# One gate product in plain fp32, and mixed rows made at another time, in the projections of an RWKV-7 layer

## The chip, the cores and the metric

The kernel runs on 1 core of one Trainium2 chip. The time is device microseconds of one execution; the median of the runs counts.

## The reference

A two-layer encoder trunk, 512 tokens by 1024 channels, in fp32: each layer is a feed-forward block, a token mixer (attention in layer 0, RWKV-7 in layer 1) and another feed-forward block. The change lies in the projections ahead of RWKV-7's scan. What they compute, cut:

```python
xx = 0.5 * (x_prev + x_next) - x
xr, xw, xk, xv, xa, xg = (x + xx * mix[i] for i in range(6))
r = xr @ w_rkv[0]; k = xk @ w_rkv[1]; v = xv @ w_rkv[2]
wl = w0 + einsum(tanh(einsum(xw, w1)), w2)          # decay, two directions
a  = sigmoid(a0 + einsum(einsum(xa, a1), a2))       # learning rate, two directions
g  = sigmoid(xg @ g1) @ g2                          # gate; g1 is 1024 x 160
kk = k * k_k / norm over each head of (k * k_k)
```

## The kernel before, in words

Everything is channel-major: 1024 channels are 8 chunks of 128 partitions, 512 tokens lie along the free axis. Large products are done as three: a matrix is split into a high half (`fp32r`, ScalarE's copy) and a low half (raw minus high, on VectorE for activations, mostly on GpSimd for weights), and `mm3` (L225 to L227) adds high x high, high x low, low x high. A few small products are plain fp32 matmuls.

`rwkv_project` works in this order, on one instruction queue per engine:

- `first` (L622 to L632), hand-ordered on ScalarE and VectorE: for each chunk VectorE adds the neighbours (`add`, L622), subtracts x (L626: `xx`) and mixes the keys' rows (L615, `mix`); ScalarE copies the high half into `xT` (L629), VectorE makes the low half (L632).
- keys: for each of 8 chunks a weight row block is loaded and split (`load_rows`, L189, L220, L221 on GpSimd) and multiplied into 8 PSUM banks, 24 products a chunk (lines L225 to L227, out `bank`, in `xT` and `ring` or `w`). TensorE's order is that of the code.
- `low_rank(0, w1, 1)` mixes the decay's rows ("w rows", L615 into `ring`), `low_rank(1, a1, 4)` the learning rate's ("a rows"); `rank(n)` (L610) multiplies each by its 1024 x 128 matrix in plain fp32.
- ScalarE evacuates each key bank (`store`, L639, into a rotation of 4 and later 8 buffers, stored to DRAM as `d_k`) and squares it (L670); L684 sums the squares by head in plain fp32 (16 columns), VectorE takes the reciprocal (L688).
- `raws(0)` mixes r's rows into the 4 `tmp` buffers (L646), stores them (`d_xr`, L647) and multiplies the first 128 columns of r (L692, plain fp32). `raws(3)` mixes v's rows and stores them (`d_xv`).
- `decays(z)` (w2, 24 products each; ScalarE L709, VectorE L710, stored as `d_lw`), between the two the gate's first product: `mixed(5)` mixes and splits the gate's rows into `xT` (L615, L220, L221), 24 `mm3` products with g1's first 128 columns and 24 with its last 32 (`g1b`).
- the gate's second product (48 products) and its stores `d_g`; then the scan begins: loads of `tri`, `k`, `iv`, `r`, `lw`, `e` (the rate's rank product from `d_ah`), with `lw` needed by the scan's first product (L1228) and `e` by its second (`ah`, L225).

Outside the hand-ordered pieces, a scheduler with its own time model orders VectorE, ScalarE, GpSimd and the DMA queue of SP; `behind(ins)` says that what is emitted in it is issued after `ins`. VectorE and SP are strict queues in the order shown below.

Of the kernel before, what the change touches and what calls it, by code (L numbers as in the profile page):

```python
# [10 lines left out]
F32 = mybir.dt.float32  # L11
BF16 = mybir.dt.bfloat16
F32R = mybir.dt.float32r
I32 = mybir.dt.int32
AF = mybir.ActivationFunctionType
ALU = mybir.AluOpType
AX = mybir.AxisListType

P = 128
# [4 lines left out]
ND = D // P  # L24
# [62 lines left out]
def halves_of(ap):  # L87
    return ap.rearrange("p (h t) -> p h t", h=2)
# [10 lines left out]
class Trunk:  # L99
# [473 lines left out]
    def rwkv_project(self, dram, xraw, w_rkv, w1, w2, a1, g1, g2, heads):  # L573

        nc = self.nc
        with self.pool("rwa") as pool:
# [9 lines left out]
            mixes = [self.new_xT()]  # L586
            rows = [[q[:, c, :] for q in (quarters(), quarters()) for c in range(4)] for _ in range(2)]
# [4 lines left out]
                ev[0] = (ev[0] + 1) % (4 * len(evs))  # L592
                return evs[ev[0] // 4][:, ev[0] % 4, :]

            def mixed(i):
                m = mixes[0]
                for c in range(ND):
                    raw = mix(i, c)
                    self.split(*m.get(c), halves_of(raw))
                return m  # L600

            def low_rank(n, w, i):
                nc.sync.dma_start(ranks[:, n], w.rearrange("(c p) f -> p c f", p=P))
                for c in range(ND):
                    mix(i, c, rows[n][c])

            def rank(n):
                pp = self.bank()
                for c in range(ND):
                    nc.tensor.matmul(pp, ranks[:, n, c, :], rows[n][c], start=c == 0, stop=c == ND - 1)  # L610
                return pp

            def mix(i, c, raw=None):
                raw = self.tmp() if raw is None else raw
                nc.vector.scalar_tensor_tensor(raw, xx[c], self.col(C_MIX + i, c),  # L615
                                               xraw[:, c, 1 : S + 1], ALU.mult, ALU.add)
                return raw

            def first(i):

                m = mixes[0]
                add = lambda c: nc.vector.tensor_tensor(xx[c], xraw[:, c, 0:S], xraw[:, c, 2 : S + 2], ALU.add)  # L622
                with self.tc.manual_schedule(engines=MANUAL_NORM):
                    add(0)
                    for c in range(ND):
                        nc.vector.scalar_tensor_tensor(xx[c], xx[c], 0.5, xraw[:, c, 1 : S + 1], ALU.mult, ALU.subtract)  # L626
                        raw = mix(i, c)
                        h, l = m.get(c)
                        hi = nc.scalar.activation(h, halves_of(raw), AF.Copy).ins  # L629
                        if c < ND - 1:  # L630
                            add(c + 1)
                        nc.vector.tensor_tensor(l, halves_of(raw), h.bitcast(F32), ALU.subtract)  # L632
                        if c == 0:
                            marks = hi, self.mark(l.bitcast(F32)[:, 0, 0:1])
                return m, marks

            def store(dst, src):
                t = evac()
# [3 lines left out]
            def raws(i, dst):  # L642

                for c in range(ND):
                    t = self.tmp()
                    self.mixed = nc.vector.scalar_tensor_tensor(t, xx[c], self.col(C_MIX + i, c), xraw[:, c, 1 : S + 1], ALU.mult, ALU.add).ins  # L646
                    nc.sync.dma_start(dst[:, c, :], t)  # L647
                    yield c, t
# [1 line left out]
            nc.sync.dma_start(heads_t, heads)  # L650
            nc.sync.dma_start(wr, w_rkv[0][:, :P].rearrange("(c p) f -> p c f", p=P))

            mk, marks = first(2)
            self.spare += kept[::-1]
            with self.behind(*marks):
                k_units += [self.load_rows(w_rkv[1], c * P, ring=True) for c in range(2, LEAD)]
                marks = self.hi, self.lo
            low_rank(0, w1, 1)
            with self.tc.manual_schedule(engines=MANUAL):
                acc = [self.bank() for _ in range(ND)]  # L660
                for c in range(ND):
                    with self.behind(*marks):
                        u = k_units[c] if c < LEAD else self.load_rows(w_rkv[1], c * P)
                    for o in range(ND):
                        self.mm3(halves_of(acc[o]), u[:, 0, o * P : (o + 1) * P], u[:, 1, o * P : (o + 1) * P],
                                 *mk.get(c), c == 0, c == ND - 1)
                sqs = [q[:, c, :] for q in (quarters(), quarters()) for c in range(4)]
                for o in range(ND):
                    store(dram["rkv"][1][:, o, :], acc[o])
                    nc.scalar.activation(sqs[o], acc[o], AF.Square, scale=self.col(C_KK, o))  # L670

                pw = rank(0)
                wt = evac()
                nc.scalar.activation(wt, pw, AF.Tanh)
                evs.append(quarters())
                wts = [evac()[: CH + 1] for _ in range(2)]
                for z in range(2):
                    nc.gpsimd.memset(wts[z][CH:], 1.0)
                    nc.sync.dma_start(wts[z][0:CH], wt[z * CH : (z + 1) * CH])
                low_rank(1, a1, 4)  # L680
                pa = rank(1)
                ss = self.bank()[:HEADS]
                for o in range(ND):
                    nc.tensor.matmul(ss, heads_t[:, o, :], sqs[o], start=o == 0, stop=o == ND - 1)  # L684
                store(dram["ah"], pa)
                iv = evac()[:HEADS]
                nc.vector.tensor_scalar(iv, ss, 1e-24, None, ALU.max)
                nc.vector.reciprocal(iv, iv)  # L688
                nc.sync.dma_start(dram["iv"], iv)
                pr = self.bank()  # L690
                for c, t in raws(0, dram["xr"]):
                    nc.tensor.matmul(pr, wr[:, c, :], t, start=c == 0, stop=c == ND - 1)  # L692
                with self.behind(self.lo, self.hi, self.mixed):
                    for z in range(2):
                        self.split(wh[z][: CH + 1, 0, :], wh[z][: CH + 1, 1, :], wts[z])
                store(dram["rkv"][0][:, 0, :], pr)
                self.spares = None
                more.__exit__(None, None, None)

                def decays(z):  # L700
                    u = self.load_unit(w2[z])
                    for t in range(NT):
                        for h in range(2):
                            pp = self.bank()
                            ws = slice(h * 512, h * 512 + 512)
                            ts = slice(t * P, t * P + P)
                            self.mm3(pp, *(wh[z][: CH + 1, i, ts] for i in range(2)), *(u[: CH + 1, i, ws] for i in range(2)), True, True)
                            th = evac()
                            nc.scalar.activation(th, pp, AF.Tanh, scale=0.5)  # L709
                            nc.vector.tensor_scalar(th, th, -0.5 * DECAY, -0.5 * DECAY, ALU.mult, ALU.add)  # L710
                            nc.sync.dma_start(dram["lw"][:, z, t, ws], th)

                mg = mixed(5)
                decays(0)
                u = self.load_cols(g1, 0)
                u2 = pool.tile([P, 2, ND, 32], F32R, name="g1b")
                raw = self.tmp()[:, : ND * 32].rearrange("p (c f) -> p c f", c=ND)
                nc.sync.dma_start(raw, g1[:, P:].rearrange("(c p) f -> p c f", p=P))
                self.split(u2[:, 0], u2[:, 1], raw)
                pg = [self.proj_cols(u, mg), self.bank()]  # L720
                for c in range(ND):
                    self.mm3(halves_of(pg[1][:32, :]), u2[:, 0, c, :], u2[:, 1, c, :], *mg.get(c), c == 0, c == ND - 1)
                gn = (P, 32)
                for i, n in enumerate(gn):
                    raw = self.tmp()[:n]
                    nc.scalar.activation(raw, pg[i][:n], AF.Tanh, scale=0.5)
                    nc.vector.tensor_scalar(raw, raw, 0.5, 0.5, ALU.mult, ALU.add)
                    self.split(gh[i][:n, 0, :], gh[i][:n, 1, :], raw)
                decays(1)
                list(raws(3, dram["xv"]))  # L730
                ug = [self.load_rows(g2, 0), self.load_unit(g2[P:, :])]
                for c in range(ND):
                    pp = self.bank()
                    for i, n in enumerate(gn):
                        cs = slice(c * P, c * P + P)
                        self.mm3(pp, ug[i][:n, 0, cs], ug[i][:n, 1, cs], gh[i][:n, 0, :], gh[i][:n, 1, :], i == 0, i == 1)
                    store(dram["g"][:, c, :], pp)
# [971 lines left out]
```

## Time and profile before

| | |
|---|---|
| median of 3 runs | 2251.94 us (2251.73 to 2253.03) |
| the profiled execution | 2249.95 us, of which the span is 2247.8 |
| TensorE busy in the span | 2173.9 us |
| mean granted TensorE clock | 0.984 |
| keys on TensorE | 1311.82 to 1362.73 us of the span |
| gate's first product | 1397.38 to 1412.21 us |
| scan's first product | 1439.61 us |

A timeline row gives start, length, engine, line, operation, out<-in, the shapes and the count merged into the row; in brackets stand the idle time of the engine just before it and what ended it. Lengths of matmuls overlap, since they are pipelined; from start to start is what one costs.

### The profile page before, as it was taken

The numbers are of one execution on the slowest core, as the hardware profiler recorded it, in microseconds if no ns is written. First come the engines' busy times: TensorE is split into PE (matmuls) and PEld (weight loads), VectorE is DVE, ScalarE is ACT, GpSimd is POOL, SyncE is SP. The second block draws the span as 40 slices with busy tenths as digits, with TensorE's granted clock in tenths as the row PEclk, the third lists the DMA queues.
The fourth block names the chain that finished last, engine by engine and source line by source line (L and its number), as shares of the span: only waits on it lengthen the run. The fifth ranks groups of instructions, "written<-read, shape, count | busy, mean of one in ns | idle before, by whom it ended". The sixth has DMA issues, their size and how long they took to land. (4 is left out here: it accounts for less than half of the span.)

```text
span 2247.8 us, 35052 instructions
## 1 busy us (share of the span) xinstructions
PE 2173.9 (97%) x13768; PEld 1707.0 (76%) x13768; DVE 1056.5 (47%) x1533; ACT 963.0 (43%) x1688; POOL 1419.6 (63%) x1235
## 2 busy tenths in 40 slices
PE   8999999999999999999999989799999998999998
PEld 7888888887888888888888865445666656888876
DVE  2333365276423333733333695434788645333345
ACT  4333345377333333543333534336767533333333
POOL 6878854555487886587877442144776722888853
PEclk9999999999999999999999989799999999999999
DMA  6444463432344445454444544764444642444443
GB/s 202 146 148 144 142 223 100 134 95 84 103 142 149 145 141 179 137 172 141 138 145 136 189 134 146 271 156 131 130 120 110 207 156 95 154 141 143 136 166 122
DMA packets 350496, 328.81 MB, mean 146 GB/s; under 512 B 48458, under 2 KB 277450, under 8 KB 350332
## 3 DMA queue, kind: packets, MB, share of 16 engines
q1 hardware_dynamic: 350332, 326.58, 46.5%
q8 instruction: 108, 1.77, 0.3%
q14 instruction: 56, 0.46, 0.1%
HBM read 262.26 MB, written 47.74 MB: 138 GB/s over the span
## 5 line engine op out<-in xcount | busy, mean ns | idle before, releaser
L221 POOL TENSOR_TENSOR w<-raw,w 128x1024 fp32r<-128x1024 f32 (+1 forms) x201 | 498.1, 2479 | 261.3 <-ACT w L220 254.5
L226 PE MATMUL bank<-xT,w 128*128 128x512 f32 x1416 | 552.1, 390 | 1.7 <-DVE xT L221 1.7
L225 PE MATMUL bank<-xT,w 128*128 128x512 f32 x1416 | 553.2, 391 | 0.0
L227 PE MATMUL bank<-xT,w 128*128 128x512 f32 x1416 | 551.9, 390 | 0.0
L220 ACT ACTIVATE w<-raw 128x1024 fp32r<-128x1024 f32 x205 | 216.5, 1059 | 335.4 <-POOL ts L779 138.0
L422 DVE SCALAR_TENSOR_TENSOR ar<-bank,tmp 128x512 f32<-128x512 f32 x88 | 60.9, 692 | 583.7 <-PE bank L227 574.5
L226 PEld LDWEIGHTS bank<-xT,w 128*128 128x128 f32 x1416 | 266.3, 188 | 56.2 <-DVE xT L221 2.6
L227 PEld LDWEIGHTS bank<-xT,w 128*128 128x128 f32 x1416 | 266.2, 188 | 55.6
L225 PEld LDWEIGHTS bank<-xT,w 128*128 128x128 f32 x1416 | 266.1, 188 | 54.3
L1376 POOL TENSOR_TENSOR tm<-qs,zs 128x126 f32<-128x126 f32 (+22 forms) x248 | 106.4, 429 | 130.5 <-DVE qs L1369 78.2
L808 PE MATMUL bank<-wx,an 128*128 128x512 f32 x792 | 187.3, 389 | 0.0
L808 PE MATMUL bank<-w,ring 128*128 128x512 f32 x720 | 170.7, 393 | 2.3 <-POOL w L221 1.7
L808 PEld LDWEIGHTS bank<-wx,an 128*128 128x128 f32 x792 | 148.7, 188 | 30.8
L221 POOL TENSOR_TENSOR wx<-ra,wx 128x512 fp32r<-128x512 f32 x132 | 166.8, 1290 | 3.1 <-ACT wx L220 3.1
L221 DVE TENSOR_TENSOR ring<-ar,ring 128x1024 fp32r<-128x1024 f32 x44 | 126.2, 2868 | 78.4 <-ACT ring L220 78.3
L808 PEld LDWEIGHTS bank<-w,ring 128*128 128x128 f32 x720 | 136.0, 189 | 32.4 <-POOL w L221 2.9
L420 ACT ACTIVATE tmp<-bank 128x512 f32<-128x512 f32 x88 | 52.6, 597 | 228.5 <-PE bank L227 228.5
L221 POOL TENSOR_TENSOR ring<-raw,ring 128x1024 fp32r<-128x1024 f32 x28 | 68.5, 2456 | 95.6 <-ACT ring L220 95.6
L1378 POOL TENSOR_TENSOR zs<-zs,tm 128x126 f32<-128x126 f32 (+22 forms) x248 | 111.4, 449 | 19.4
L225 PE MATMUL bank<-xT,ring 128*128 128x256 f32 (+1 forms) x352 | 104.6, 305 | 10.4 <-ACT xT L220 3.9
L221 POOL TENSOR_TENSOR w<-late,w 128x1024 fp32r<-128x1024 f32 x30 | 75.5, 2523 | 61.5 <-ACT w L220 61.5
L220 ACT ACTIVATE wx<-ra 128x512 fp32r<-128x512 f32 x132 | 82.9, 633 | 72.2 <-PE bank L808 67.9
(279 smaller groups left out, 3746.4 us busy)
## 6 DMA issues: line engine op xcount, KB each, us to landing
raw<-in_ffn_w_in_dram SPq DMA_DIRECT2D x176, 512.0 KB, 3.9
ra<-in_ffn_w_out_dram SPq DMA_DIRECT2D x44, 1024.0 KB, 5.0
late<-d_late SPq DMA_DIRECT2D x34, 512.0 KB, 5.2
late<-in_ffn_w_out_dram SPq DMA_DIRECT2D x28, 512.0 KB, 4.7
raw<-in_w_qkv_dram SPq DMA_DIRECT2D x24, 512.0 KB, 3.9
d_late<-ts SPq DMA_DIRECT2D x44, 256.0 KB, 3.3
d_late<-ra SPq DMA_DIRECT2D x44, 256.0 KB, 2.0
xs<-ar SPq DMA_DIRECT2D x64, 128.0 KB, 2.4
```

Of the source, the lines that this page charges most:

```text
L220: self.hi = self.nc.scalar.activation(h, raw, AF.Copy).ins
L221: self.lo = (eng or self.nc.vector).tensor_tensor(l, raw, h.bitcast(F32), ALU.subtract).ins
L225: nc.tensor.matmul(out, wh, xh, start=start, stop=False)
L226: nc.tensor.matmul(out, wh, xl, start=False, stop=False)
L227: nc.tensor.matmul(out, wl, xh, start=False, stop=stop)
L420: nc.scalar.activation(s, pg, AF.Silu)
L422: nc.vector.scalar_tensor_tensor(raw[:, 3:7:3] if j else raw[:, 0:8:7], halves_of(pu), 0.5, halves_of(s), ALU.mult, ALU.mult)
L808: self.nc.tensor.matmul(acc, lhs, u[:, i], start=bool(first) and m == 0, stop=last and m == 2, skip_group_check=more)
L1376: nc.gpsimd.tensor_tensor(tv, qs[:, s, 0:s].rearrange("p (a o) -> p a o", o=1).broadcast_to([P, s, n]), zs[:, s : s + 1, c0:].broadcast_to ...
L1378: nc.gpsimd.tensor_tensor(zs[:, 0:s, c0:], zs[:, 0:s, c0:], tv, ALU.add)
```

## The change

The gate's rows are no longer split. `low_rank(0, g1[:, :P], 5)` mixes them into the buffers of the w rows, once the decay's rank product has read those, and `rank` does the gate's first product: 8 plain fp32 matmuls with 128 columns and 8 with 32. `mixed` goes, and so do the splits of g1. The w rows, a rows and v rows are emitted behind `ends`, the last low half of `first`; the a rows and v rows are emitted right after the keys' products, where before the a rows came after the decay's rank product and the v rows after `decays(1)`.

```diff
-            def mixed(i):
-                m = mixes[0]
+            def low_rank(n, w, i, *ins):
+                nc.sync.dma_start(ranks[:, n], w.rearrange("(c p) f -> p c f", p=P))
+                with self.behind(*ins):
+                    for c in range(ND):
+                        mix(i, c, rows[n][c])
+
+            def rank(n, w=None):
+                pp = self.bank()
+                w = ranks[:, n] if w is None else w
                 for c in range(ND):
-                    raw = mix(i, c)
-                    self.split(*m.get(c), halves_of(raw))
-                return m
-
-            def low_rank(n, w, i):
-                nc.sync.dma_start(ranks[:, n], w.rearrange("(c p) f -> p c f", p=P))
-                for c in range(ND):
-                    mix(i, c, rows[n][c])
-
-            def rank(n):
-                pp = self.bank()
-                for c in range(ND):
-                    nc.tensor.matmul(pp, ranks[:, n, c, :], rows[n][c], start=c == 0, stop=c == ND - 1)
+                    nc.tensor.matmul(pp[: w.shape[2]], w[:, c, :], rows[n][c], start=c == 0, stop=c == ND - 1)
                 return pp
...
-                        nc.vector.tensor_tensor(l, halves_of(raw), h.bitcast(F32), ALU.subtract)
+                        lo = nc.vector.tensor_tensor(l, halves_of(raw), h.bitcast(F32), ALU.subtract).ins
...
-                return m, marks
+                return m, marks, lo
...
-            mk, marks = first(2)
+            mk, marks, ends = first(2)
...
-            low_rank(0, w1, 1)
+            low_rank(0, w1, 1, ends)
             with self.tc.manual_schedule(engines=MANUAL):
...
+                low_rank(1, a1, 4, ends)
+                with self.behind(ends):
+                    list(raws(3, dram["xv"]))
...
-                low_rank(1, a1, 4)
+                low_rank(0, g1[:, :P], 5)
+                g1b = pool.tile([P, ND, 32], F32, name="g1b")
+                nc.sync.dma_start(g1b, g1[:, P:].rearrange("(c p) f -> p c f", p=P))
                 pa = rank(1)
...
-                mg = mixed(5)
                 decays(0)
-                u = self.load_cols(g1, 0)
-                u2 = pool.tile([P, 2, ND, 32], F32R, name="g1b")
-                raw = self.tmp()[:, : ND * 32].rearrange("p (c f) -> p c f", c=ND)
-                nc.sync.dma_start(raw, g1[:, P:].rearrange("(c p) f -> p c f", p=P))
-                self.split(u2[:, 0], u2[:, 1], raw)
-                pg = [self.proj_cols(u, mg), self.bank()]
-                for c in range(ND):
-                    self.mm3(halves_of(pg[1][:32, :]), u2[:, 0, c, :], u2[:, 1, c, :], *mg.get(c), c == 0, c == ND - 1)
+                pg = [rank(0), rank(0, g1b)]
...
                 decays(1)
-                list(raws(3, dram["xv"]))
```

How the change moves instructions is shown at three places. First VectorE in the loop of `first`, from chunk 3's mix to chunk 4's low half (`ring<-ring,cols,xraw` are w rows, `xT<-tmp,xT` a chunk's low half). Before:

```order
L615 SCALAR_TENSOR_TENSOR tmp<-ring,cols,xraw 128x512
L622 TENSOR_TENSOR ring<-xraw 128x512
L615 SCALAR_TENSOR_TENSOR ring<-ring,cols,xraw 128x512 x4
L632 TENSOR_TENSOR xT<-tmp,xT 128x2x256
L626 SCALAR_TENSOR_TENSOR ring<-ring,xraw 128x512
L615 SCALAR_TENSOR_TENSOR tmp<-ring,cols,xraw 128x512
L622 TENSOR_TENSOR ring<-xraw 128x512
L615 SCALAR_TENSOR_TENSOR ring<-ring,cols,xraw 128x512
L632 TENSOR_TENSOR xT<-tmp,xT 128x2x256
```

and now, from chunk 7's mix to what follows the loop (the chunks before it have the same four rows each and nothing between them; L641 `x10` are 8 v rows and 2 r rows, and the last `ring` rows the gate's):

```order
L610 SCALAR_TENSOR_TENSOR tmp<-ring,cols,xraw 128x512
L627 TENSOR_TENSOR xT<-tmp,xT 128x2x256
L610 SCALAR_TENSOR_TENSOR ring<-ring,cols,xraw 128x512 x16
L641 SCALAR_TENSOR_TENSOR tmp<-ring,cols,xraw 128x512 x10
L610 SCALAR_TENSOR_TENSOR ring<-ring,cols,xraw 128x512
L641 SCALAR_TENSOR_TENSOR tmp<-ring,cols,xraw 128x512
L610 SCALAR_TENSOR_TENSOR ring<-ring,cols,xraw 128x512
L641 SCALAR_TENSOR_TENSOR tmp<-ring,cols,xraw 128x512
L610 SCALAR_TENSOR_TENSOR ring<-ring,cols,xraw 128x512 x6
L687 TENSOR_SCALAR ring<-bank 16x512
```

So the w rows stand behind the whole loop, and a rows, v rows, half of the r rows and the gate's rows between it and the reciprocal.

Second SP's queue while the keys end, from the load of w2 on (`raw<-in_w_dram`), up to the store of `d_ah`. Now:

```order
L642 DMA d_xv<-tmp 128x512 x2
L189 DMA raw<-in_g_dram 128x1024
L642 DMA d_xv<-tmp 128x512 x4
L635 DMA d_k<-ring 128x512 x2
L642 DMA d_xv<-tmp 128x512 x2
L635 DMA d_k<-ring 128x512
L642 DMA d_xr<-tmp 128x512
L635 DMA d_k<-ring 128x512
L642 DMA d_xr<-tmp 128x512
L635 DMA d_k<-ring 128x512
```

Before, four `d_xr` stores stood ahead of the first `d_k` and no `d_xv` at all; now six `d_xv` stand ahead of it, and the fourth `d_k` is behind an `d_xr`.

Third SP at the scan's start, where the scan's first product waits for the first `lw`. Before:

```order
L1205 DMA a2r<-in_a_dram 128x2x128
L1223 DMA r<-d_r 128x512
L1225 DMA lw<-d_lw 128x4x128
L1104 DMA mask<-in_smask_dram 128x256
L1104 DMA onesb<-in_onesb_dram 128x128
L1099 DMA e<-d_ah 128x512
```

and now:

```order
L1196 DMA a2r<-in_a_dram 128x2x128
L1090 DMA e<-d_ah 128x512
L1214 DMA r<-d_r 128x512
L1216 DMA lw<-d_lw 128x4x128
L1095 DMA mask<-in_smask_dram 128x256
```

The load of `e` has moved ahead of `r` and `lw`, the rest keeps its order.

## The prediction

> **What bounds the kernel now.** I read the page's header and engine row first, then busy time by stage around the change (a row: stretch, length, busy time and count of PE, PEld, DVE, ACT and POOL, granted clock, DMA share, GB/s), then TensorE's (PE's) timeline there.
>
> ```profile
> span 2247.8 us, 35052 instructions
> PE 2173.9 (97%) x13768; PEld 1707.0 (76%) x13768; DVE 1056.5 (47%) x1533; ACT 963.0 (43%) x1688; POOL 1419.6 (63%) x1235
> ```
>
> ```profile
> 1318.25:1340.00 21.75, 19.55 (x79) 15.69 (x78) 21.64 (x18) 5.83 (x8) 13.78 (x5) 0.92 0.19 61
> 1397.40:1412.20 14.80, 13.10 (x49) 7.93 (x48) 12.76 (x19) 6.89 (x12) 9.71 (x4) 0.88 0.37 121
> ```
>
> TensorE is busy 97% of the span, so what the change can win is TensorE's work and its holes in this one stage. In these two stretches (keys; gate) it has holes and a granted clock below 1, while VectorE (DVE) is nearly full: there VectorE sets the end.
>
> **The keys.** PE's rows around chunk 3 of the keys (24 products from 1331.41; chunk 4 begins at 1340.97):
>
> ```profile
> 1331.41 0.39 PE L225 MATMUL bank<-xT,ring 128*128 128x512 f32 x1
> 1334.00 0.50 PE L226 MATMUL bank<-xT,ring 128*128 128x512 f32 x1 [2.21 <-DVE xT L632]
> ...
> 1335.26 0.59 PE L225 MATMUL bank<-xT,ring 128*128 128x512 f32 x1
> ...
> 1338.90 0.39 PE L225 MATMUL bank<-xT,ring 128*128 128x512 f32 x1
> ...
> 1340.97 0.39 PE L225 MATMUL bank<-xT,w 128*128 128x512 f32 x1
> ```
>
> Nine products from 1338.90 to 1340.97 give 0.23 us a product, so 24 should take 5.5; they take 9.56. Of the 4.0 lost, 2.4 are the wait for chunk 3's low half, and 1.6 the nine products from 1335.26 to 1338.90 at 0.40. VectorE and GpSimd (POOL) show why the half is late:
>
> ```profile
> 1314.58 0.69 DVE L632 TENSOR_TENSOR xT<-tmp,xT 128x512 fp32r<-128x512 f32 x1
> ...
> 1317.36 0.69 DVE L632 TENSOR_TENSOR xT<-tmp,xT 128x512 fp32r<-128x512 f32 x1
> ...
> 1318.69 2.78 DVE L615 SCALAR_TENSOR_TENSOR tmp<-ring,cols,xraw 128x512 f32<-128x512 f32 x1
> ...
> 1324.20 9.14 DVE L615 SCALAR_TENSOR_TENSOR ring<-ring,cols,xraw 128x512 f32<-128x512 f32 x4
> 1333.27 0.68 DVE L632 TENSOR_TENSOR xT<-tmp,xT 128x512 fp32r<-128x512 f32 x1
> ```
>
> ```profile
> 1318.35 5.38 POOL L221 TENSOR_TENSOR ring<-raw,ring 128x1024 fp32r<-128x1024 f32 x2 [5.22 <-ACT ring L220]
> 1323.69 8.44 POOL L221 TENSOR_TENSOR w<-raw,w 128x1024 fp32r<-128x1024 f32 x3
> ```
>
> While GpSimd splits weights (2.7 to 2.8 us each, until 1332.1), a VectorE operation of 0.7 us takes as long as one split. The four w rows of the decay (L615 x4) spend three such slots ahead of chunk 3's low half. The change puts them behind the whole loop. Then the slots from 1324.20 go to chunk 3's low half (done 1327.0, due 1331.6) and chunk 4's subtraction and mix (1332.6). An undisturbed step is 2.78 in all (1314.58 to 1317.36); its second half, ScalarE's (ACT) copy and the low half, follows, so chunk 4 is ready by 1334.0, at the very latest 1335.4, and due at 1331.41 + 5.5 = 1336.9. Later chunks need 2.78 of VectorE against 5.5 on PE. So wait and slow products both go: **-4.0**; keys end at 1358.7 instead of 1362.73.
>
> **The gate's first product.** Before, 48 split products; after, 16 plain fp32 ones. The fp32 prices are in the same stage: the ranks, and the head sums with 16 columns.
>
> ```profile
> 1397.38 0.40 PE L225 MATMUL bank<-xT,w 128*128 128x512 f32 x1
> ...
> 1401.58 0.50 PE L226 MATMUL bank<-xT,w 128*128 128x512 f32 x1 [1.07 <-DVE xT L221]
> ...
> 1403.18 0.50 PE L226 MATMUL bank<-xT,w 128*128 128x512 f32 x1 [0.64 <-DVE xT L221]
> 1403.51 0.58 PE L227 MATMUL bank<-xT,w 128*128 128x512 f32 x1
> ...
> 1407.15 0.40 PE L227 MATMUL bank<-xT,g1b 128*32 128x512 f32 x1
> ...
> 1412.21 0.40 PE L225 MATMUL bank<-w,ring 65*128 65x512 f32 x1
> ```
>
> ```profile
> 1362.73 13.89 PE L610 MATMUL bank<-ring 128*128 128x512 f32 x32
> 1376.55 7.04 PE L684 MATMUL bank<-ring,heads 128*16 128x512 f32 x16
> ...
> 1388.38 3.70 PE L692 MATMUL bank<-tmp,wr 128*128 128x512 f32 x8 [1.16 <-DVE tmp L646]
> ```
>
> Before: 1397.38 to 1412.21 is 14.83 = 48 x 0.23 (11.0) + 2.2 waiting for mixed rows + 1.6 slow (nine products from 1403.51 to 1407.15). After: 16 rank products take two records each, 1362.73 to 1376.55, so 8 cost 6.91; 8 narrow ones cost 7.0 by the head sums' row (16 columns; fewer columns save nothing). Together 13.9: **-0.95**. Without the slow stretch before would be 13.3, and the new form loses 0.6.
>
> The Trainium skill ("FP8 and Floating Point Precision", TensorE Precision Notes) gives true fp32 four passes and so speaks against this edit: estimated at 0.23 a pass, 14.7 instead of 13.9. The trace has 0.864 a product, 3.8 passes, so the measured row stands in the sum.
>
> **Moved work, at nothing.** From 1342.3 VectorE has 8 w, 8 a and 8 v mixes. The nearest row, eight mixes with one split among them, gives 0.94 each:
>
> ```profile
> 1351.09 7.52 DVE L615 SCALAR_TENSOR_TENSOR ring<-ring,cols,xraw 128x512 f32<-128x512 f32 x8
> ```
>
> The w rows are ready at 1350 (needed 1358.7), the a rows at 1357.4 (needed 1365.6), the v rows at 1365 (needed in the scan). The g rows take the w rows' place once the first rank has read them (1365.6) and have until 1393. Keys and ranks on PE are the cover; without it, 0.94 a mix. PE's wait inside the r product (1.16) follows the head sums and their reciprocal in both orders: it stays. The removed splits on ScalarE, VectorE and GpSimd lay beside other work: 0. On SP, g1's narrow part is now loaded ahead of the last x store, which nothing needs before the scan: 0.
>
> **The scan's start.** SP now issues e (the rate's rows) ahead of lw, on which PE's first product waits:
>
> ```profile
> 1435.45 0.43 SPq L1225 DMA_DIRECT2D lw<-d_lw  x1
> ...
> 1436.95 0.43 SPq L1099 DMA_DIRECT2D e<-d_ah  x1
> ```
>
> ```profile
> 1439.61 2.05 PE L1228 MATMUL a<-tri,lw 128*128 128x128 f32 x8 [7.62 <-DMA mask<-in_smask_dram]
> 1441.92 0.79 PE L225 MATMUL a<-ah,a2u 128*128 128x512 f32 x1 [0.27 <-ACT ah L220]
> 1442.64 0.79 PE L226 MATMUL a<-ah,a2u 128*128 128x512 f32 x1
> ```
>
> lw goes out 0.5 later with 256 KB more in front (0.8 at 328 GB/s, the rate of a row below), but the next product no longer waits for ah, which gives back 0.3 to 0.5. Bounds -0.3 and +0.8; I take **+0.3**.
>
> **Sum** against the profiled execution (2249.95 for a span of 2247.8): -4.0 - 0.95 + 0.3 = -4.7, so 2245.3. The median of the runs, 2251.94, is 2.0 above that execution.
>
> **What is chance in it.** In stretches of 3.41 us counted from 1335.24:
>
> ```profile
> 1331.83:1335.24 3.41, 1.24 (x5) 1.05 (x6) 3.38 (x5) 0.00 (x0) 0.30 (x1) 1.00 0.00 0
> 1335.24:1338.66 3.42, 3.42 (x10) 2.62 (x9) 3.38 (x7) 0.67 (x2) 0.00 (x0) 0.51 0.00 0
> ...
> 1400.09:1403.51 3.42, 1.72 (x6) 0.78 (x5) 3.42 (x8) 1.72 (x4) 3.23 (x1) 1.00 1.00 328
> 1403.51:1406.92 3.41, 3.41 (x10) 2.33 (x9) 2.80 (x3) 0.64 (x2) 3.05 (x1) 0.51 0.31 94
> ...
> 1543.45:1546.87 3.42, 1.82 (x24) 1.49 (x24) 3.25 (x6) 2.30 (x6) 3.03 (x6) 1.00 0.76 230
> 1546.87:1550.28 3.41, 3.18 (x31) 2.06 (x31) 2.74 (x8) 1.93 (x4) 2.86 (x8) 1.00 0.50 159
> ```
>
> Each slow stretch fills exactly one cell of this grid (20 cells lie between the two), after a cell with PE busy 1.72 or less; after 1.82 none follows. I know of nothing in the program that sets where the grid lies. So a slow cell needs some 1.64 idle within one cell. The keys' wait (2.21 idle) does that for (3.41 + 2.21 - 2 x 1.64) / 3.41 = 0.69 of the grid's places. The gate's 1.71 is spread over 2.67, so for (3.41 - 2.67 + 0.14) / 3.41 = 0.26, all of them among the former. This profile has both. So of executions before the change, about 0.26 have both slow cells (gain 4.7), 0.43 the keys' alone (4.0 - 0.6 - 0.3 = 3.1), 0.31 neither (1.5).
>
> The Trainium skill ("TensorE: Matmul & The Clock Gate", What's actually happening) says the same: a window of 3413 ns, free-running, half clock after an idle one. The two slow cells agree; by it the 4.7 of this profile isn't each execution's.
>
> **Rivals.**
> - *Both slow cells in most runs*: 2251.94 - 4.7 = 2247.2. For it: the profile; against: the 0.26.
> - *Neither*: 2250.4. Against: 2.21 idle is well over 1.64.
> - *Slower: the keys' stores queue behind the v rows.* SP now has six v stores ahead of the first key store; ScalarE's last four evacuations wait for key stores 0 to 3, and the last head sum needs the eighth's square. Three landings follow one another: v row 1 frees a tmp for row 5, row 5 for r row 1, and key store 3, queued behind r row 1, frees the eighth's buffer.
>
> ```profile
> d_k<-ring SPq DMA_DIRECT2D x8, 256.0 KB, 4.4
> d_xr<-tmp SPq DMA_DIRECT2D x4, 256.0 KB, 2.1
> ...
> wv<-in_w_rkv_dram SPq DMA_DIRECT2D x1, 512.0 KB, 6.7
> ```
>
> At 2.1 a landing: v rows begin at 1357.4, row 5 is issued by 1362, r row 1 mixed at 1365, key store 3 lands by 1368.5, copy and square follow: 1370, due 1378.6 (head sums start at 1372.5, the last 6.1 later). Three longer landings add up: at 4.4 it is 1376.9, still in time; at 6.7, the slowest row, 1383.8: PE waits 5.2, and 2251.94 - 3.1 + 5.2 = 2254.0. It decides from 6.0 a landing, where the wait takes the whole gain. For it: 20 stores and a 512 KB load in some 15 us are 370 GB/s, above the 328 of the row. Against: only half of it lies ahead of key store 3.
> - *The change doesn't do it: the wait moves to chunk 4.* If VectorE gets two slots fewer between the splits, chunk 4 is as late as chunk 3 was, and only the gate's loss stays: 2251.94 + 0.6 + 0.3 = 2252.8. Against: 2.9 us to spare, a whole slot, and it takes two.
>
> **How the numbers follow.** Keys' cell alone 0.40, both 0.26, neither 0.20, queued stores 0.07, wait at chunk 4 0.07. Forecast: 2251.94 - 3.1 = **2248.8**, its own range 2247.3 to 2250.3. The range 2245.8 to 2252.8 takes in both, neither and the scan's bounds. 0.2% is 4.5 us, about what a measurement of this kernel can tell from no change: faster is below 2247.4 (half of "both", a little of the forecast: 0.25), slower above 2256.4 (the stores' far end: 0.07), the rest 0.68.
>
> **What would show it.** After: no wait of PE on the low halves in the keys, and a granted clock of 1 there; the gate's first product 13.9 without a hole; head sums unbroken; the scan's first product some 4.7 earlier. Wrong would be a PE wait at chunk 4, in the head sums, or at the second gate rank, or a scan that starts as late as before.

## The result, and the profile after

The changed kernel takes **2241.22 us** (median of five runs, 2239.96 to 2246.83) against 2251.94 for the kernel before beside it (2251.36 to 2253.92): a ratio of 0.9966, 95% interval 0.995 to 0.9982. Two later comparisons gave 0.9962 (0.9949 to 0.9975) and 0.9968 (0.9958 to 0.9978). So by the three ratios it is 7 to 9 us faster, with intervals from 4 to 11. The two medians of the first comparison lie further apart, 10.7 us (0.9952). The forecast was 2248.8, its range 2245.8 to 2252.8: the time lies outside. The profiled execution took 2241.22 us.

```profile
span 2239.4 us, 35001 instructions
PE 2171.0 (97%) x13752; PEld 1702.8 (76%) x13752; DVE 1065.7 (48%) x1524; ACT 959.1 (43%) x1678; POOL 1412.8 (63%) x1234
```

The two stretches of the prediction, at their new places (the keys begin 1.56 us later in this execution): TensorE is busy all the time in both, at a granted clock of 1. (A row: stretch, length, busy time and count of PE, PEld, DVE, ACT and POOL, granted clock, DMA share, GB/s.)

```profile
1319.81:1341.56 21.75, 21.75 (x98) 18.01 (x97) 21.26 (x17) 6.47 (x9) 13.79 (x5) 1.00 0.20 61
1393.70:1407.70 14.00, 14.00 (x34) 4.56 (x32) 1.98 (x4) 2.90 (x5) 2.34 (x1) 1.00 0.22 82
```

**The keys.** TensorE's chunk 3 begins at 1331.49 and chunk 4 (operand `w`) at 1336.93, 5.44 us, with nothing waited for; VectorE has chunk 3's low half in the slot that starts at 1325.76, and chunk 4's is done at 1335.7.

```profile
1331.49 0.39 PE L225 MATMUL bank<-xT,ring 128*128 128x512 f32 x1
1331.72 0.39 PE L226 MATMUL bank<-xT,ring 128*128 128x512 f32 x1
...
1336.93 0.39 PE L225 MATMUL bank<-xT,w 128*128 128x512 f32 x1
```

```profile
1325.76 2.88 DVE L627 TENSOR_TENSOR xT<-tmp,xT 128x512 fp32r<-128x512 f32 x1
...
1331.49 2.77 DVE L610 SCALAR_TENSOR_TENSOR tmp<-ring,cols,xraw 128x512 f32<-128x512 f32 x1
...
1335.02 0.69 DVE L627 TENSOR_TENSOR xT<-tmp,xT 128x512 fp32r<-128x512 f32 x1 [0.16 <-ACT xT L624]
```

GpSimd still splits five weights in the same place as before, and VectorE still spends one slot on each; the slots now go to the keys' own rows:

```profile
1319.92 5.36 POOL L221 TENSOR_TENSOR ring<-raw,ring 128x1024 fp32r<-128x1024 f32 x2 [5.22 <-ACT ring L220]
1325.25 8.46 POOL L221 TENSOR_TENSOR w<-raw,w 128x1024 fp32r<-128x1024 f32 x3
```

**Ranks, head sums, r, gate** (TensorE; L605 is `rank`, L684 the head sums, L692 the r product): all begin as soon as the one before ends, except the r product's second half; the gate's first product runs from 1393.73 to 1407.67, **13.94 us**.

```profile
1358.69 13.89 PE L605 MATMUL bank<-ring 128*128 128x512 f32 x32
1372.52 7.04 PE L684 MATMUL bank<-ring,heads 128*16 128x512 f32 x16
1379.49 3.70 PE L692 MATMUL bank<-tmp,wr 128*128 128x512 f32 x8
1384.74 3.70 PE L692 MATMUL bank<-tmp,wr 128*128 128x512 f32 x8 [1.55 <-DVE tmp L641]
...
1393.73 7.03 PE L605 MATMUL bank<-ring 128*128 128x512 f32 x16
1400.69 7.05 PE L605 MATMUL bank<-ring,g1b 128*32 128x512 f32 x16
1407.67 0.50 PE L225 MATMUL bank<-w,ring 65*128 65x512 f32 x1
```

**The queue of stores.** On SP the v rows (L642) go out ahead of the first key store (L635), as the rival of that name had it, and ScalarE waits 11.81 us for a buffer.

```profile
1361.77 1.01 SPq L642 DMA_DIRECT2D d_xv<-tmp  x2
...
1363.38 2.66 SPq L642 DMA_DIRECT2D d_xv<-tmp  x4
1366.14 1.47 SPq L635 DMA_DIRECT2D d_k<-ring  x2
```

```profile
1358.08 0.71 ACT L668 ACTIVATE ring<-bank,cols 128x512 f32<-128x512 f32 x1
1370.60 0.60 ACT L634 ACTIVATE ring<-bank 128x512 f32<-128x512 f32 x1 [11.81 <-DMA d_k<-ring]
...
1375.48 0.68 ACT L668 ACTIVATE ring<-bank,cols 128x512 f32<-128x512 f32 x1
```

The last square is done at 1376.2; the head sums begin at 1372.52 and need it 6.1 later, at 1378.6. It was 2.4 us from costing something.

**The scan's start** (TensorE), changed, and then the second row's counterpart before:

```profile
1436.83 2.05 PE L1219 MATMUL a<-tri,lw 128*128 128x128 f32 x8 [9.23 <-DMA lw<-d_lw]
...
1450.59 3.65 PE L989 MATMUL y<-az,xs 128*64 128x512 f32 x16 [0.47 <-DMA xs<-in_w_rkv_dram]
```

```profile
1455.50 3.65 PE L998 MATMUL y<-az,xs 128*64 128x512 f32 x16 [1.43 <-DMA xs<-in_w_rkv_dram]
```

From the gate's end to the scan's first product it is 29.16 us (before 27.40): 1.76 later. From there to the product of L989 it is 13.76 (before 1439.61 to 1455.50, 15.89): 2.1 earlier. The two cancel. In the means of three profiles of each kernel it is 2.0 later and then 2.5 earlier.

**The account**, from TensorE's starts in three profiles of each kernel (before: the one shown, before2, before3; changed: the one shown, same, same2), in us:

| | before | changed | mean difference |
|---|---|---|---|
| keys' first product to the first rank | 50.9, 50.7, 50.8 | 45.3, 46.9, 45.6 | -4.9 |
| first rank to the gate's first product's end | 49.5, 49.3, 49.3 | 49.0, 48.6, 48.8 | -0.6 |
| all the rest of the span | 2147.4, 2146.3, 2149.3 | 2145.1, 2146.2, 2144.8 | -2.3 |

The sum, -7.8, agrees with the three ratios (-7.2 to -8.6 of 2250). The last row is the least certain: the three profiles before spread by 3.0 us there.

The first row needs a second look. The keys begin in a half-speed stretch of the clock, whose length differs from profile to profile, so their first chunk of 24 products takes 7.2 to 8.8 us. Where the wait for chunk 3 exists this doesn't matter: a longer start leaves a shorter wait. The rows of the wait, in before2 (first chunk 7.95) and in rows, a kernel of the next section (first chunk 7.29), beside the 2.21 of the prediction's profile (first chunk 8.71):

```profile
1336.55 0.80 PE L226 MATMUL bank<-xT,ring 128*128 128x512 f32 x1 [2.96 <-DVE xT L632]
```

```profile
1334.95 0.50 PE L226 MATMUL bank<-xT,ring 128*128 128x512 f32 x1 [3.60 <-DVE xT L633]
```

First chunk and wait together are 10.9 us in all seven profiles that have the wait: VectorE sets that moment. So 2.21 was the shortest wait of the seven, because that start was the longest. Without the wait the length of the start counts in full.

### The profile page after: what moved, and what is told of

It reads as the page before. It is cut to its first block, busy times and chain, and to the rows that moved or that the text cites. A ratio compares the mean times of both kernels' runs of the same rounds, so it can differ in the third digit from the quotient of the medians.

```text
span 2239.4 us, 35001 instructions
## 1 busy us (share of the span) xinstructions
PE 2171.0 (97%) x13752; PEld 1702.8 (76%) x13752; DVE 1065.7 (48%) x1524; ACT 959.1 (43%) x1678; POOL 1412.8 (63%) x1234
## 5 line engine op out<-in xcount | busy, mean ns | idle before, releaser
L221 POOL TENSOR_TENSOR w<-raw,w 128x1024 fp32r<-128x1024 f32 x200 | 490.3, 2453 | 247.7 <-ACT w L220 236.2
L225 PE MATMUL bank<-xT,w 128*128 128x512 f32 x1408 | 549.6, 390 | 0.0
L227 PE MATMUL bank<-xT,w 128*128 128x512 f32 x1408 | 548.2, 389 | 0.0
L220 ACT ACTIVATE w<-raw 128x1024 fp32r<-128x1024 f32 (+1 forms) x204 | 215.4, 1058 | 333.8 <-POOL ts L770 141.9
L227 PEld LDWEIGHTS bank<-xT,w 128*128 128x128 f32 x1408 | 264.4, 188 | 55.2
L225 PEld LDWEIGHTS bank<-xT,w 128*128 128x128 f32 x1408 | 264.5, 188 | 53.8
L221 DVE TENSOR_TENSOR ring<-ar,ring 128x1024 fp32r<-128x1024 f32 x44 | 133.4, 3032 | 76.3 <-ACT ring L220 76.2
L221 POOL TENSOR_TENSOR ring<-raw,ring 128x1024 fp32r<-128x1024 f32 x28 | 68.3, 2449 | 94.8 <-ACT ring L220 94.8
L225 PE MATMUL bank<-xT,ring 128*128 128x256 f32 (+1 forms) x352 | 104.2, 304 | 9.3 <-ACT xT L220 3.4
```

The source lines that it names most:

```text
L220: self.hi = self.nc.scalar.activation(h, raw, AF.Copy).ins
L221: self.lo = (eng or self.nc.vector).tensor_tensor(l, raw, h.bitcast(F32), ALU.subtract).ins
L225: nc.tensor.matmul(out, wh, xh, start=start, stop=False)
L227: nc.tensor.matmul(out, wl, xh, start=False, stop=stop)
```

## The experiments

Each kernel's edit is given against the kernel before or the changed one. Single executions of one kernel scatter by up to 12 us (the kernel before: 2243.4 to 2255.3 in 30 runs), so ratios with their intervals count. A half-speed cell is one stretch of 3.41 us of the prediction's grid with a granted clock of 0.5.

**same**, the changed kernel once more.

> The changed kernel once more, nothing edited. Its five runs lay in two groups (2240.0 to 2241.2 and 2245.8 to 2246.8), its profile in the lower. Theory 1 (the change wins in its own stage only, and the rest of the difference is where half-speed clock cells happen to fall): times spread again over about 2240 to 2247, since the cells fall anew in each execution, and a profile of another time differs from the first one in whole cells of about 1.7 us each, not in waits. Theory 2 (the change also shortens the scan by moving the v stores out of its way): the scan from its first product on takes the same time in every profile, some 2 to 3.5 us less than before the change.

Measured: 2241.47, ratio 0.9962 (0.9949 to 0.9975). Six runs from 2237.1 to 2244.6, no two groups. Theory 1 has the scatter, but not the size: its stage gain of some 5 us lies just outside the interval (5.6 to 11.5).

**keys, gate, rows**: each part alone.

```diff
keys:  -            low_rank(0, w1, 1)
       +            low_rank(0, w1, 1, ends)
gate:  -                mg = mixed(5)
       +                low_rank(0, g1[:, :P], 5)
       ...
       +                pg = [rank(0), rank(0, g1b)]
rows:  +                low_rank(1, a1, 4, ends)
       +                with self.behind(ends):
       +                    list(raws(3, dram["xv"]))
```

> The kernel before with one edit: the four to eight mixes of the decay's rows wait for the last low half of the keys. Theory 1: the keys lose TensorE's wait of 2.4 us and, where it fell there, a half-speed cell of 1.6: the profile shows no wait of TensorE on a low half, and the median is 2.4 to 4.0 us under that of the kernel before (2248 to 2249.5). Theory 2 says the same of this part, and that the scan's length is that of the kernel before. A rival: the lost time comes back in the head sums or the ranks, then the median stays at 2252.

> The kernel before with one edit: the gate's first product in plain fp32, its rows mixed in place, with the keys and the v and a rows as before. Theory 1: the product takes 13.9 us instead of 14.8 in a profile with a slow cell there and 13.3 in one without, so the median moves by -0.9 to +0.6 us (2251 to 2252.5). Theory 2 expects no more of it. A rival: the removed copies and splits on VectorE and ScalarE let the decays or the gate's second product end earlier, which would give 1 us or more beyond that, seen in the stretch from the gate's end to the scan's first product.

> The kernel before with one edit: the rows of the learning rate and of the values are mixed, and the latter stored, while the keys are computed; the decay's rows still go ahead of the keys' chunk 3, and the gate stays in split products. Theory 1: no change, 2252 within 1 us, since that work lay beside other work in both places. Theory 2: the scan is shorter by 2 to 3.5 us, and the median is 2248.5 to 2250. A rival: the eight stores ahead of the key stores make TensorE wait in the head sums, then 2253 or more.

Measured: keys 2251.08, ratio 1.0003 (0.9995 to 1.0012); gate 2248.19, 0.9989 (0.9979 to 0.9999); rows 2254.54, 1.0022 (1.0013 to 1.0031). The parts alone add up to +1.4 per thousand; together they give -3.5. They act on one another. (One piece of the change is in none of the three: gate emits the mixes of the gate's rows behind the r product, the changed kernel ahead of the second rank product.) Keys alone shows how. TensorE's wait for chunk 3 is gone, and in its place it waits for a bank at the first rank (TensorE, ScalarE and SP of keys; L640 is the key banks' evacuation there):

```profile
1363.48 16.26 PE L611 MATMUL bank<-ring 128*128 128x512 f32 x32 [4.33 <-ACT ring L671]
```

```profile
1361.31 1.06 ACT L220 ACTIVATE w<-raw 128x1024 fp32r<-128x1024 f32 x1 [11.62 <-DMA raw<-in_g_dram]
1362.27 0.58 ACT L640 ACTIVATE ring<-bank 128x512 f32<-128x512 f32 x1
```

```profile
1343.72 12.50 SPq L648 DMA_DIRECT2D d_xr<-tmp  x4
1356.32 0.39 SPq L189 DMA_DIRECT2D raw<-in_g_dram  x1
```

ScalarE has the copy of the gate's columns ahead of the first evacuation; its load stands on SP behind four stores of r rows, the last of which is mixed only after the w rows. The bank comes 4.3 us late, and two half-speed cells fall there. In rows the same copy makes TensorE wait 3.17 us at the first rank; its load stands behind a v row's store there.

**gate_keys** (the edits of gate and of keys together), **late_v** (the changed kernel with the v rows back behind `decays(1)`), **gate_rows** (the changed kernel with `low_rank(0, w1, 1)` without `ends`), **before2**.

```diff
late_v:   -                with self.behind(ends):
          -                    list(raws(3, dram["xv"]))
          ...
                          decays(1)
          +                list(raws(3, dram["xv"]))
```

> The kernel before with two parts of the change: the gate's first product in fp32, and the decay's rows behind the last low half of the keys; the a and v rows stay where they were. With the second part alone TensorE waited 4.3 us for its first free bank, because the copy of the gate's weight columns stood ahead of the keys' evacuations on ScalarE and its load was queued behind the r rows' stores. Theory A (the parts need each other): here that copy does not exist, so no wait of that kind, and the median is 5 to 6 us under the kernel before: about 2 from the gate, 2.4 from the keys' wait and 1 or so from half-speed cells: 2244 to 2245.5. Theory B (the rest of the gain comes from the order of the scan's transfers, which the moved v stores change): only -2 to -4, 2246 to 2248. Plain adding up of the parts measured alone: 2249.

> The changed kernel with the v rows mixed and stored where they were before, between the decays; the a rows stay early. The scan's transfers are then again in the order of before (e behind lw, the reloads of az and xs as before). Theory A: same as the changed kernel within 1.5 us (2240 to 2243.5). Theory B: 3 us or more slower than the changed kernel (2244.5 or more), with the time lost after the scan's first product.

> The changed kernel without the wait of the decay's rows for the last low half: they are mixed ahead of chunk 3 again. Theory A: TensorE's wait for chunk 3 returns (2.4 us), and another weight's copy (the gate's second product) now stands ahead of the keys' evacuations on ScalarE with its load behind the v stores on SP, so TensorE also waits for its first bank, 3 us or more: 2247 or more. Theory B: 2244 to 2246 (only the keys' wait comes back).

> The kernel before once more, for a second profile. If the half-speed cells fall anew in each execution, its cells lie elsewhere than in the first profile (in that one: the keys' chunk 3, the gate, and one at the end of the last layer), while TensorE's wait of 2.2 to 2.4 us for chunk 3 and its 1.7 us of waits in the gate are there again. If they are tied to the program, the same cells return.

Measured: gate_keys 2243.91, ratio 0.9984 (0.9972 to 0.9995): theory A's median came, but its cause was named wrongly. Without the gate's copy, the copy of a w2 half stands in its place, its load again behind the r stores, and TensorE still waits 2.99 us for a bank. late_v 2243.24, 0.9969 (0.9957 to 0.9981): as the changed kernel, and no wait for a bank: in its order the w2 load stands ahead of the last r store again. So nothing is seen that the v rows give, or the order of the scan's first transfers that goes with them, and theory B's 3 us or more aren't there by the ratios; but the interval (4.3 to 9.7 us under the kernel before) can't tell 2 us from nothing. gate_rows took 2247.59 in its one run: the wait for chunk 3 is back (3.44 us), but not the wait for a bank that theory A had as well. before2 took 2248.36 with the wait for chunk 3 (2.96 us) and a half-speed cell behind it, none in the gate, none at the end of the last layer. It shows the gate's first product undisturbed (L225 to L227 into `w` and `g1b`; 1414.39 is the next product):

```profile
1399.77 0.40 PE L225 MATMUL bank<-xT,w 128*128 128x512 f32 x1
...
1403.95 0.50 PE L226 MATMUL bank<-xT,w 128*128 128x512 f32 x1 [1.05 <-DVE xT L221]
...
1405.55 0.50 PE L226 MATMUL bank<-xT,w 128*128 128x512 f32 x1 [0.64 <-DVE xT L221]
...
1409.29 0.42 PE L227 MATMUL bank<-xT,g1b 128*32 128x512 f32 x1 [1.16 <-DVE g1b L221]
...
1414.39 0.40 PE L225 MATMUL bank<-w,ring 65*128 65x512 f32 x1
```

At full clock it takes **14.62 us**, not 13.3. The third wait, for the low half of `g1b`, had been covered by the half-speed cell of the first profile.

**same2, no_gate, gate_load, iv_late.** no_gate is the changed kernel with the split gate; gate_load is gate with one load of the gate's columns more; iv_late is the changed kernel with one wait more on VectorE.

```diff
gate_load: +                self.load_cols(g1, 0)
iv_late:   -                nc.vector.tensor_scalar(iv, ss, 1e-24, None, ALU.max)      (ahead of the r rows)
           +                with self.behind(self.mixed):                               (behind them)
           +                    nc.vector.tensor_scalar(iv, ss, 1e-24, None, ALU.max)
```

> The changed kernel once more, beside the next three. Theory A (all of the gain is in the stage from the keys to the gate, some 5 us by three profiles, and the rest of the two measured differences of 8.7 is how the half-speed cells fell): 4 to 6 us under the kernel before in this call. Theory C (there is a steady gain of 3 to 4 us outside the stage as well): 8 to 10 us under it again.

> The changed kernel with the gate's first product as before, in split products: the decay's rows behind the last low half, and the a and v rows early. In its program the copy of the gate's columns stands ahead of the keys' evacuations again, but its load now goes out ahead of the v stores. Theory A (what matters is whether that load is queued behind row stores): no wait of TensorE for a bank, the keys' gain of 2.4 to 4.5 us is there, and the median is 3.5 to 5 us under the kernel before. Rival (the copy itself, wherever its load is queued, makes TensorE wait 3 to 4 us): the median is that of the kernel before or more. Theory C, if the steady gain comes from the gate's products: no more than theory A says.

> The fp32 gate alone (2 to 2.5 us under the kernel before, of which its product explains 0.7), and the weight unit of the gate's wide columns is loaded, copied and split at the place where it was before, though nothing reads it: work added. Theory A: 0.7 us under the kernel before, like the fp32 gate alone, within 1.5. Theory C, if the steady gain comes from one weight unit less (one buffer fewer in the turn, one load and one split fewer): the gain beyond 0.7 goes away here and stays in the fp32 gate alone. TensorE should not wait for it: 0 either way in the keys.

> The changed kernel, and the reciprocal of the head sums (0.7 + 3.3 us of VectorE) goes behind the last four r rows instead of ahead of them. TensorE waits 1.16 us for the fifth r row in both kernels, put down to that order. If so, the wait goes (product and its rows are 0.9 and 0.75 us each), and the time falls by 1.2 us against the changed kernel of the same call, a little under what such a comparison can tell; the profile shows it. Rival: the decay's splits that wait behind the last r row and the reciprocal start the decays later, and nothing is won.

Measured: same2 2241.72, ratio 0.9968 (0.9958 to 0.9978), between the two theories. no_gate 2248.01, 0.9995 (0.9985 to 1.0005): its stage has all of the keys' gain (94.8 us from the keys' first product to the gate's end, before 100.0 to 100.4) and no wait for a bank, and yet nothing is won: it loses it 390 us later, where the scan's end waits for its output weights (`wv`):

```profile
1788.10 1.97 PE L1000 MATMUL a<-wv,xv 128*64 128x512 f32 x4 [5.77 <-DMA wv<-in_rw_out_dram]
```

In rows it is 5.23 there; in before 0.48, in the changed kernel 1.38. gate_load 2244.35, 0.9983 (0.997 to 0.9995): as gate alone within the intervals, so there is no sign that one load, copy and split less was worth anything; they lay beside other work. iv_late 2240.52, 0.9958 (0.9943 to 0.9973): the r product runs in one piece,

```profile
1381.61 7.13 PE L688 MATMUL bank<-tmp,wr 128*128 128x512 f32 x16
```

and from the head sums' start to the decays TensorE needs 1.4 to 1.6 us less (13.54) than in same and same2, where it waits 1.16 and 1.35. By its median it is the fastest of all kernels here; its interval overlaps that of the changed kernel beside it.

**pad, wv_last, before3.** Spare products after the gate's last one, which nothing reads:

```diff
+                pd = self.bank()
+                for i in range(32):
+                    nc.tensor.matmul(pd[:, :2], ug[0][:, 0, :P], gh[0][:, 0, :2], start=True, stop=True)
```

(wv_last: 64 columns for 2.)

> The changed kernel with 32 spare products of 2 columns (nothing reads them) between the gate's last product and the scan, where TensorE waits 9 us anyway: about as many TensorE instructions as the fp32 gate saves. The load wv keeps its place. Theory D (the hole near 1825 us is a stall for instructions, whose place depends on how many stand before it): the hole of 0.4 to 1.0 us comes back, and the time is 1 to 2 us above the changed kernel (whose comparisons gave -7.6 to -9.6 against the kernel before). Rival (the hole belongs to the split gate in another way): no hole, same time as the changed kernel.

> As pad, but the spare products have 64 columns, which lets the scheduler place the load wv at the end of the scan behind three other loads of 512 KB, as in the two kernels with early rows and the split gate; nothing else in any engine's order differs from pad. Theory E (that place alone costs what those two lost): TensorE waits 5 to 6 us for wv instead of about 1, and the time is 4 to 6 us above pad. Rival (the wait there came from the v rows' stores or the gate's loads): a wait of 1 to 2 us and the time of pad.

> The kernel before, a third profile. If the hole without a wait near 1825 us is steady or frequent in it (in one of two profiles so far) it shows again; the wait for wv is 0.5 to 1.2 us; the gate's first product takes 14.6 us if no half-speed cell falls into it, not 13.3 as the prediction had it.

Measured: pad 2244.82, ratio 0.9979 (0.9968 to 0.999); wv_last 2252.83, 1.0018 (1.0008 to 1.0029). The loads at the scan's end in SP's order, and the product that needs `wv`, in pad and then in wv_last:

```profile
1775.33 0.54 SPq L1492 DMA_DIRECT2D bk<-in_rw_out_dram  x1
1775.96 0.39 SPq L1483 DMA_DIRECT2D wv<-in_rw_out_dram  x1
1776.41 0.42 SPq L1494 DMA_DIRECT2D xs<-in_rw_out_dram  x1
1777.08 0.33 SPq L1483 DMA_DIRECT2D ar<-in_rw_out_dram  x1
1777.45 0.50 SPq L1494 DMA_DIRECT2D xs<-in_rw_out_dram  x1
```

```profile
1780.77 1.98 PE L992 MATMUL a<-wv,xv 128*64 128x512 f32 x4
```

```profile
1777.88 0.54 SPq L1494 DMA_DIRECT2D xs<-in_rw_out_dram  x1
1778.51 0.39 SPq L1492 DMA_DIRECT2D bk<-in_rw_out_dram  x1
1778.96 0.42 SPq L1494 DMA_DIRECT2D xs<-in_rw_out_dram  x1
1779.62 0.33 SPq L1483 DMA_DIRECT2D ar<-in_rw_out_dram  x1
1780.04 0.48 SPq L1483 DMA_DIRECT2D wv<-in_rw_out_dram  x1
```

```profile
1788.18 1.97 PE L992 MATMUL a<-wv,xv 128*64 128x512 f32 x4 [5.32 <-DMA wv<-in_rw_out_dram]
```

Five loads of 512 KB go out within 2.2 us; second of five `wv` is there in time, last of five it is 5.3 us late, and the kernel is 8.0 slower (by the medians): the wait, and half-speed cells from 1784 on (three, in pad one). Theory E holds; its price was set too low. That place is what rows and no_gate paid for: in their programs, too, the scheduler puts `wv` last. The changed kernel keeps it second.

pad has the hole without a wait again, and larger:

```profile
1815.83 0.70 PE L1410 MATMUL p<-qd,qc 32*32 32x32 f32 x33
1819.01 0.31 PE L1410 MATMUL p<-qd,qc 32*32 32x32 f32 x3 [2.48 <-issue]
```

wv_last has it too (1.86). That is theory D's sign, but pad isn't clean: it also reorders a few transfers, and at the scan's start it waits 2.73 us for `xs` where the changed kernel waits 0.47. before3 took 2251.46; it has the wait for chunk 3 (2.91) and a cell behind it, no hole, 2.02 of wait for `wv` (more than the 0.5 to 1.2 expected), and the gate's first product takes 14.68.

## Why the prediction was wrong

- **Keys, -4.0: the mechanism right, the term too small.** The w rows' slots were the cause, and both the wait and the slow products go: -4.9 in three profiles. The wait was priced by one profile, whose 2.21 was the shortest of seven (2.21 to 3.60), since its keys had the longest half-speed start. Also without the slow cell the wait doesn't stay at 2.4, as "neither" had it: in rows and gate_load, which have no cell there, it is 3.60. Chunk 4's low half was done at 1335.7, as worked out (1334.0, and the keys begin 1.56 later here); it was needed at 1337.16, so 1.4 us were to spare, not 2.9. The chance of a half-speed cell behind this wait (0.69) fits: five of the seven profiles that have the wait have the cell.
- **The gate's first product: the step whose reasoning failed.** "Without the slow stretch before would be 13.3, and the new form loses 0.6" took the slow cell's 1.6 off a sum that VectorE bounded. Without the cell TensorE only came sooner to the next split and waited there: 14.61 to 14.68 in the five profiles of split gates without the cell (before2, before3, keys, rows, no_gate), against 13.94 to 13.95 in all eleven with the fp32 gate. So the term is -0.7 in nearly every execution, where the forecast used +0.6. That moves the forecast by 1.3. One of six has the cell, near the 0.26 that was worked out.
- **Moved work at nothing: right for this kernel, and luckier than the working knew.** The terms were priced one by one and added. Alone, two of the three parts give nothing or cost 5 us, by the bank that came late and by `wv`. Which loads stand behind which stores on SP was looked at for the key stores only, not for the weight loads between them.
- **The scan's start, +0.3: wrong in itself (1.76, outside the bounds of -0.3 and +0.8; why so much wasn't traced), right in the sum,** since 2.1 come back by the next loads.
- **The sum stopped at the scan's start.** Some 2.3 us more lie in the rest of the span; the prediction gave it no term. What the rest can do is shown by wv_last: 8 us, from an order 350 us behind the edit. What of it the changed kernel gains stays open; `wv` isn't it, for its load stands second before and after. The fp32 gate is a candidate: gate alone gained 0.0011 (interval 0.0001 to 0.0021) and gate_load 0.0017 (0.0005 to 0.003), of which its product explains 0.0003; the first interval takes that in, so a further gain isn't shown. late_v speaks for neither the v rows nor the order of the scan's first transfers. The half-speed cells between 1455 and 2220 us don't settle it (7, 4 and 7 before, 6, 5 and 5 in the changed kernel). The hole near 1825 is in three of six profiles with the split gate and in none of nine with the fp32 gate and no spare products, but two of the changed kernel's three profiles have one of 0.40 and 0.47 us some 50 us earlier.
- **The base.** The forecast counted from 2251.94, the median of the kernel before beside the first comparison. In the four later ones, of 21 to 30 runs each, that kernel took 2248.7 to 2250.1, while the changed kernel stayed at 2241.5 and 2241.7. If that is the kernel's usual time, 2 to 3 us of the distance between 2248.8 and 2241.22 are this base; why the first comparison's five executions lay higher isn't known. The rest of the distance is 0.9 of the keys, 1.3 of the gate and the rest of the span.
- **The rivals.** The queued stores came within 2.4 us of TensorE. The wait at chunk 4 stayed away by 1.4. "Both slow cells" (2247.2) was the nearest case; it had the gate's term nearly right (-0.95), and the time is below it by the base, the keys' 0.9 and the rest of the span.

## What to carry to other kernels

A slow stretch of the clock can't be subtracted from a stage where another engine sets the pace: the time turns into waiting there. Ahead of a wait it costs nothing, as the keys' start did; behind it, it costs its full 1.6. Ask of it what a second profile without the stretch would show. Where a scheduler places the loads, a moved row or a few spare instructions can reorder weight loads hundreds of us later: compare the whole order of the DMA queue, not only the stage, and price which load stands last. Parts of one change that were each tried alone don't add up when they share a strict queue: ScalarE's copies wait for loads, loads for stores, stores for VectorE's rows.

## What the runs showed of the hardware

- A VectorE operation on 128x512 fp32 that takes 0.69 us alone took 2.77 to 2.88 in the keys while GpSimd split weights of 128x1024 (2.7 to 2.8 us each): five splits from 1319.92 to 1333.71 in the changed kernel, and five such operations from 1320.26 to 1334.26.
- Half-speed stretches last 3.41 us or a whole multiple of it in every profile, but for the last, which the end of the span cuts; their places differ from one execution to the next. The Trainium skill ("TensorE: Matmul & The Clock Gate", What's actually happening) gives a free-running window of 3413 ns. The traces agree. How much idle time brings one is less clear than the prediction had it (1.64 us within one cell): the waits of 3.60 us in rows and gate_load, which the grid cuts into 1.8 to 1.9 and 1.7 to 1.8, had none behind them, while those that lay with 2.05 us or more in one cell (before2 and before3 2.6, gate 2.4, gate_rows 2.05) had. Yet in the gate's product before, 1.69 of idle time in one cell (busy 1.72 of 3.41) had one too, so no single threshold fits all.
- Plain fp32 at 128x512 costs 0.87 us a product with 128 columns as with 32 (13.94 to 13.95 for 16, in eleven profiles).
- TensorE stops for 0.4 to 2.5 us near the scan's end without any wait that the profile shows, in some executions only. Its place differs between kernels (a product of `bk` near 1826 in keys, one of `qd` at 1819 in pad and near 1775 in two profiles of the changed kernel). Whether it waits for instructions there isn't settled.
